# Output products of the first block in pairs, its next operands kept in DRAM unsplit

## The chip, the cores and the metric

The kernel runs on one core of a Trainium2 chip. The metric is the device time of one execution in microseconds (us). Before the change it is 2675.44 us, the median of three runs (2669.7 to 2675.79).

## The reference, cut to what matters

Two blocks follow each other on 512 tokens of 2048 features, all in f32. The first block has two layers; the second has one, with 16 meta tokens ahead of the 512.

```python
for l in range(DEPTH):                       # DEPTH = 2
    h = rmsnorm(x, attn_norm_g[l])
    proj = h @ w_in[l]
    qa, ka, va, ga, cq, ckv, kr, gb = jnp.split(proj, SPLIT_POINTS, axis=-1)
    ya = swa_attention(...) * jax.nn.silu(ga)
    yb = mla_attention(cq, ckv, kr, ...) * jax.nn.silu(gb)
    x = x + jnp.concatenate([ya, yb], axis=-1) @ w_out[l]
return rmsnorm(x, final_norm_g)
...
```

The second block takes that result, normalises it, multiplies by a second input matrix (gates, attention operands, pooling), and ends with a product by a second output matrix.

## The kernel before, in words

**Tiles and products.** Features lie on the 128 partitions, so an activation of 2048 features is 16 operand tiles c of 128x512. A weight tile is 128x1024 in f32: the weights of one output tile t for eight operand tiles (one half u). SP loads it into `wr` (three buffers, or `ws`, two buffers, for weight sums). `load_w_split` (L246) makes two fp32r parts of it: ACT casts it to `wh` (L249), DVE subtracts to get `wl` (`tt`, L129), three buffers each. Every operand is split the same way, and every product is three matmuls: hi by `wh`, lo by `wh`, hi by `wl` (`mm3`, L160). A plain output tile is 2 halves x 8 operands x 3 = 48 matmuls of 512 columns.

**Pairs.** `run_pair` (L346) makes two output tiles at once from seven products of half the columns (8 operands x 3 matmuls each, 168 matmuls of 256 columns), named z, x and y, in place of eight. It needs weight sums, which POOL's accumulating DMAs put into DRAM (`wsd`, `sum_step`, L224, each held back behind a PE instruction), and for each of the eight pairs of operands (n, n+8) an operand set (`t_set`, L327): four half-width operations on DVE and two splits. The sets come from a side task (`t_build`), which reloads the unsplit operands as `tr`. Before the change pairs stand in the second block's input product, except for the first eight gate tiles (`GPLAIN`), and in its output product w_out2 (five pairs).

**The order of the work.** PE runs in the order that the program writes: products, with side tasks (attention heads, norms, operand sets) stepped in between by a clock that counts PE's work. The instructions of the other engines are put in order by a list scheduler, apart from the start, whose order is written by hand. Each engine then works its queue in order. A weight load on SP waits for the split three weight tiles earlier, since that frees its buffer; that split waits for PE to be done with the tile three before it.

**A layer of the first block** (`layer`, L784): the products of w_in in the order cq (three tiles as a group, both halves), ckv, and so on; attention as side tasks; then the product by w_out in 16 output tiles j, the first three as a group. After tile j, DVE adds the old x (`xo`, loaded by SP) to give `xn`, SP stores it, ACT squares it and POOL adds the square up, and the next stage's operand is made at once from `xn`: in layer 0 `hh` (ACT) and `hl` (DVE), in layer 1 `Xh`, `Xl` and an unsplit copy `xr` in DRAM. After the last tile the squares are summed over the partitions by two matmuls (`csum`, from `csh` and `csl`), 33 matmuls into the next stage. In between SP loads `metas` (the meta tokens), whose squares `mq` ACT makes ahead of `csh`.

**The start** is 16 loads of x, a split of each (`hh`, `hl`), a square of each on ACT (`x0q`), which POOL adds up as it comes, and the column sum 111 matmuls into cq, which has 144.

Of the kernel before, what the change touches and what calls it, by code (L numbers as in the profile page):

```python
# [18 lines left out]
P = 128  # L19
# [21 lines left out]
GPLAIN = 8  # L41
# [6 lines left out]
SUMPAIRS = 37  # L48
# [56 lines left out]
def trunk_kernel(ctx, tc, xT, w_in, w_qkv, w_out, w_in2, w_pool, w_aup, w_pup, w_out2, metaT, vec, cst, outT):  # L105
# [283 lines left out]


# [53 lines left out]
    cos_t = slot("cos_t")  # L444
    sin_t = slot("sin_t")
    delta_t = slot("delta_t", F32, 256)
    diag_t = slot("diag_t")
# [3 lines left out]
    def load_consts1():  # L451
        nc.sync.dma_start(cos_t, cst[:, C_COS:C_COS + S])
        nc.sync.dma_start(sin_t, cst[:, C_SIN:C_SIN + S])
        nc.sync.dma_start(delta_t, cst[:, C_DELTA:C_DELTA + 256])
        nc.sync.dma_start(diag_t, cst[:, C_DIAG:C_DIAG + S])

    xrd = tc.dram_tile([P, NC, W], F32, name="xrd")
    xd = [tc.dram_tile([P, NC, S], F32, name=f"xd{i}") for i in range(2)]
# [33 lines left out]
    def swa_pair(i, qps, r, st, nsink, gate, ydst):  # L492
# [10 lines left out]
        for kv in range(2):  # L503
            nc.gpsimd.tensor_scalar(al[:, kv * 256:(kv + 1) * 256], delta_t, -SLOPES[kv * 8 + i], None, op0=ALU.mult)
# [87 lines left out]
    def rope_of(ps, name):  # L592
# [3 lines left out]
        tt(a, ps, cos_t, ALU.mult)  # L596
        for q in range(4):
            src = slice(32 * q, 32 * q + 32)
            d = 32 * (q ^ 1)
            tt(b[d:d + 32], ps[src], sin_t[src], ALU.mult)  # L600
# [50 lines left out]
    def mla_head(h, pr, kr, gate, ydst):  # L651
# [8 lines left out]
        for i in range(NB):  # L660
# [6 lines left out]
            nc.vector.tensor_tensor_reduce(p[:, :n], sc[:, :n], diag_t[:, S - n:], -MLA_SCALE, 1e38, ALU.add, ALU.min,  # L667
# [45 lines left out]
    def plan():  # L713
        for lay in range(DEPTH):
# [17 lines left out]
            for j in range(GRP, NC):  # L732
                for u in range(2):
                    wq.append((w_out[lay, j, u], WCOLS))
        t = 0
        pairs = []
# [47 lines left out]
    def layer(lay, h, rd, x_src, x_dst):  # L784
# [15 lines left out]
        def yget(c):  # L800
            if ys[c] is None:
                need(lambda: y[c] is not None)
                ys[c] = split(y[c], f"y{c}")
                y[c] = None
            return ys[c]
# [46 lines left out]
        res = []  # L852
        for j in range(NC):
            xo = slot("xo")
            nc.sync.dma_start(xo, x_src[:, j, :])
            if j == 0:
                first = run_gemm(2, 8, yget, group=GRP)
            ps = first[j] if j < GRP else run_gemm(2, 8, yget)
            xn = slot("xn")
            tt(xn, ps, xo, ALU.add)  # L860
            nc.sync.dma_start(x_dst[:, j, :], xn)
            sq.add(xn)
            if lay == 0:
                res.append(split_g(xn, vcol(V_ATTN_G + NC * (lay + 1) + j), "h"))
            else:
# [4 lines left out]
                hi = slot("Xh", F32R, W)  # L870
                lo = slot("Xl", F32R, W)
                xr = slot("xr", F32, W)
                nc.scalar.mul(real(xr), halves(xg), g2)
                nc.scalar.mul(halves(xr)[:, :, :M2], halves(metas[:, j * NM:(j + 1) * NM]), g2)
                nc.scalar.dma_start(xrd[:, j, :], xr)
                nc.scalar.mul(real(hi), halves(xg), g2)
                stt(real(lo), halves(xg), g2, real(f32(hi)), ALU.mult, ALU.subtract)
                mt = halves(metas[:, j * NM:(j + 1) * NM])
                nc.scalar.mul(halves(hi)[:, :, :M2], mt, g2)
                stt(halves(lo)[:, :, :M2], mt, g2, halves(f32(hi))[:, :, :M2], ALU.mult, ALU.subtract)  # L880
                res.append((hi, lo))
# [35 lines left out]
    sq0 = SumSq("x0")  # L917
    h = []
    xs = []
    with tc.manual_schedule(engines={mybir.EngineType.Activation, mybir.EngineType.DVE, mybir.EngineType.SP}):  # L920
# [4 lines left out]
        def x_use(c):  # L925
            h.append(split_g(xs[c], vcol(V_ATTN_G + c), "h"))

# [13 lines left out]
        for c in range(1, 4):  # L941
            x_use(c)
            sq0.add(xs[c - 1])
        for c in range(4, 8):
            x_use(c)
            sq0.add(xs[c - 1])
        load_w_split(*raw1)
        for c in range(8, 12):
            x_use(c)
            sq0.add(xs[c - 1])  # L950
        load_w_split(*raw2)
        for c in range(12, NC):
            x_use(c)
            sq0.add(xs[c - 1])
# [534 lines left out]
```

## Time and profile before

| what | value |
|---|---|
| median of three runs | 2675.44 us |
| the profiled execution | 2675.18 us |
| its span | 2673.4 us |
| mean granted clock of PE | 0.992 |
| busy: PE, DVE, ACT, POOL | 98%, 68%, 50%, 19% |
| DMA engines' share, bytes | about 5 tenths, 163 GB/s |
| chain that ended last, by engine | PE 92%, DVE 3%, DMA 2% |

The profiled execution's time is 1.8 us more than its span. Busy shares are means over stages that differ: the products by w_in and w_out run with PE busy all the time, and the idle 2% of PE lies in a few places, at the start, at a layer's end and in the second block. Times inside the profile count from the span's start.

### The profile page before, as it was taken

What the parts mean: (1) busy time and instruction counts of PE and PEld (TensorE: products, weight loads), DVE (VectorE), ACT (ScalarE), POOL (GpSimd) and SP (SyncE); (2) the same over time, 40 slices, a digit from 0 to 9 for tenths busy, and PEclk for the clock granted to TensorE, in tenths of its full rate; (3) what the DMA queues carried; (4) which work ended last, traced back from release to release, by engine and by line L of the source; (5) the groups of instructions that cost most, each with busy time, mean ns of one, the idle gap of its engine ahead of it and who ended that gap; (6) DMA issues with size and microseconds to landing.
All of it is one profiled execution on the core that took longest, in us unless ns stands there. A gap on an engine that the chain in (4) does not pass through costs nothing.

```text
span 2673.4 us, 39297 instructions
## 1 busy us (share of the span) xinstructions
PE 2622.8 (98%) x15169; PEld 2296.0 (86%) x15169; DVE 1804.9 (68%) x2699; ACT 1323.7 (50%) x2192; POOL 513.5 (19%) x501
## 2 busy tenths in 40 slices
PE   7999999999999999999999999999999998999997
PEld 6888888888788888888888999999999986878797
DVE  7767576744467657765466787777777665766786
ACT  5444465532245445555445444335666575733453
POOL 4112123222121212323420122000000031210012
PEclk9999999999999999999999999999999998999998
DMA  5445545577764554458864455545545534466555
GB/s 180 111 145 143 134 119 150 135 218 212 185 160 120 135 138 127 130 146 235 232 187 139 152 178 163 157 159 158 159 154 167 174 115 159 154 215 208 195 175 181
DMA packets 146330, 434.71 MB, mean 163 GB/s; under 512 B 16592, under 2 KB 21072, under 8 KB 146144
## 3 DMA queue, kind: packets, MB, share of 16 engines
q1 hardware_dynamic: 103136, 306.36, 35.6%
q0 software_dynamic: 27312, 97.20, 15.9%
q10 hardware_dynamic: 15696, 28.65, 3.1%
q8 instruction: 119, 1.95, 0.3%
q14 instruction: 67, 0.55, 0.1%
HBM read 382.60 MB, written 127.14 MB: 191 GB/s over the span
## 4 chain that ended last, share of the span: by engine, by line
PE 92%; DVE 3%; DMA 2%; ACT 1%; issue 1%; POOL 1%; ACTq 0%; SPq 0%; DVEq 0%; POOLq 0%
PE mm L160 52%; PE y L160 12%; PE x L160 8%; PE z L160 8%; PE msc L160 1%; PE qn L160 1%; PE sc L160 1%; PE mo L160 1%; PE o L160 1%; PE tp L164 1%; PE kn L160 1%; PE v L160 1%; PE mtp L164 1%; DVE wl L129 1%; PE qr L160 1%
## 5 line engine op out<-in xcount | busy, mean ns | idle before, releaser
L249 ACT CAST wh<-wr 128x1024 fp32r<-128x1024 f32 (+2 forms) x448 | 462.0, 1031 | 683.8 <-PE mm L160 398.8
L129 DVE TENSOR_TENSOR wl<-wr,wh 128x1024 fp32r<-128x1024 f32 (+2 forms) x448 | 568.3, 1272 | 247.5 <-ACT wh L249 234.2
L160 PE MATMUL mm<-hh,wh 128*128 128x512 f32 x1024 | 410.8, 401 | 6.9 <-ACT wh L249 6.6
L160 PE MATMUL mm<-hh,wl 128*128 128x512 f32 x1024 | 405.1, 396 | 4.3 <-DVE wl L129 4.2
L160 PE MATMUL mm<-hl,wh 128*128 128x512 f32 x1024 | 404.9, 395 | 2.7 <-DVE hl L132 2.7
L160 PEld LDWEIGHTS mm<-hh,wl 128*128 128x128 f32 x1024 | 193.4, 189 | 50.5 <-DVE wl L129 5.9
L160 PEld LDWEIGHTS mm<-hh,wh 128*128 128x128 f32 x1024 | 193.8, 189 | 42.8 <-ACT wh L249 6.6
L227 POOL DMA_DIRECT2D wsd<-in_w_in x128 | 88.3, 690 | 732.2 <-PE mm L160 501.3
L160 PEld LDWEIGHTS mm<-hl,wh 128*128 128x128 f32 x1024 | 193.8, 189 | 39.9 <-DVE hl L132 4.6
L249 ACT CAST wh<-ws 128x1024 fp32r<-128x1024 f32 x111 | 116.4, 1048 | 151.9 <-PE y L160 99.8
L160 PE MATMUL y<-t34h,wh 128*128 128x256 f32 (+1 forms) x592 | 167.1, 282 | 0.0
L160 PE MATMUL y<-t34l,wh 128*128 128x256 f32 (+1 forms) x592 | 166.7, 282 | 0.0
L160 PE MATMUL y<-t34h,wl 128*128 128x256 f32 (+1 forms) x592 | 166.6, 281 | 0.0
L129 DVE TENSOR_TENSOR wl<-ws,wh 128x1024 fp32r<-128x1024 f32 x111 | 138.9, 1251 | 21.9 <-ACT wh L249 19.4
L160 PE MATMUL x<-Xl,wh 128*128 128x256 f32 (+1 forms) x512 | 144.6, 282 | 0.0
L160 PE MATMUL x<-Xh,wh 128*128 128x256 f32 (+1 forms) x512 | 144.4, 282 | 0.0
L160 PE MATMUL x<-Xh,wl 128*128 128x256 f32 (+1 forms) x512 | 144.3, 282 | 0.0
L160 PEld LDWEIGHTS y<-t34h,wh 128*128 128x128 f32 x592 | 111.4, 188 | 0.2 <-issue 0.2
L160 PEld LDWEIGHTS y<-t34l,wh 128*128 128x128 f32 x592 | 111.5, 188 | 0.0
L160 PEld LDWEIGHTS y<-t34h,wl 128*128 128x128 f32 x592 | 111.4, 188 | 0.0
L160 PE MATMUL mm<-Xh,wh 128*128 128x512 f32 x256 | 101.9, 398 | 0.0
L160 PE MATMUL mm<-Xh,wl 128*128 128x512 f32 x256 | 100.9, 394 | 0.0
(1023 smaller groups left out, 7057.6 us busy)
## 6 DMA issues: line engine op xcount, KB each, us to landing
wr<-in_w_in SPq DMA_DIRECT2D x256, 512.0 KB, 3.7
wsd<-in_w_in POOLq DMA_DIRECT2D x128, 512.0 KB, 5.3
wr<-in_w_out SPq DMA_DIRECT2D x95, 512.0 KB, 4.6
ws<-wsd SPq DMA_DIRECT2D x37, 512.0 KB, 4.0
wr<-wsd SPq DMA_DIRECT2D x37, 512.0 KB, 3.8
wsd<-in_w_out POOLq DMA_DIRECT2D x20, 512.0 KB, 5.7
xd<-xn SPq DMA_DIRECT2D x32, 256.0 KB, 4.5
sgd<-sga ACTq DMA_DIRECT2D x32, 256.0 KB, 2.2
```

What stands on the lines that cost most here:

```text
L129: nc.vector.tensor_tensor(out, a, b, op)
L160: last_pe[0] = nc.tensor.matmul(out, a, b, start=start, stop=stop, skip_group_check=True).ins
L164: nc.tensor.transpose(out, x, ident)
L227: behind_pe(nc.gpsimd.dma_start(dst, src, **kw))
L249: nc.scalar.copy(hi, raw)
```

## The change

It has five parts. (1) The w_out product of both layers: tiles 0 to 2 as a group, 3 plain, 4 to 13 as five pairs, 14 and 15 plain. Its unsplit operands y are stored to DRAM (`yd`, by POOL) when they are split, and reloaded by `t_build`, now shared by all users, with a shorter yield. (2) The next stage's operands 0 to 13 are stored unsplit (`raw` to `hrd` or `xrd`, by ACT), reloaded by SP as `rr` (eight during tile 14, six during tile 15) and split then. The sum x is written into `xo`. (3) The squares of the input are added on DVE later, the first addition behind a matmul of the cq group; the column sum moves from 111 matmuls into cq to behind all 144. (4) Six plain gate tiles instead of eight. (5) Constants (`cos`, `sin`, `delta`, `diag`) are loaded again at the end of layer 0, which frees their slots before, and `metas` after them.

```diff
-GPLAIN = 8
+GPLAIN = 6
-SUMPAIRS = 37
+SUMPAIRS = 48
...
+    def t_build(ts, get, raw, w):
+        ahead = {}
+        def fetch(n):
+            if n < 8:
+                ahead[n] = []
+                for c in (n, n + 8):
+                    get(c)
+                    ahead[n].append(load(raw[:, c, :], "tr", w))
+        fetch(len(ts))
+        yield 3000
+        while len(ts) < 8:
+            n = len(ts)
+            fetch(n + 1)
+            ts.append(t_set(get(n), get(n + 8), *ahead.pop(n)))
+            yield 6500
...
+        def tile_done(j, xn):
             nc.sync.dma_start(x_dst[:, j, :], xn)
             sq.add(xn)
+            raw = slot("raw", F32, w)
             if lay == 0:
-                res.append(split_g(xn, vcol(V_ATTN_G + NC * (lay + 1) + j), "h"))
+                nc.scalar.mul(raw, xn, vcol(V_ATTN_G + NC + j))
...
+            if lay == 1 or j < NC - 2:
+                nc.scalar.dma_start(rawd[:, j, :], raw)
+            if j >= NC - 2:
+                res[j] = split(raw, "h", w)
+        ts = []
+        start_side(t_build(ts, yget, yd[lay], S))
...
+        for j in range(GRP):
+            xo_load(j)
+        for j, ps in enumerate(run_gemm(2, 8, yget, group=GRP)):
+            plain_out(j, ps)
+        for j in range(GRP, NPLAIN):
+            xo_load(j)
+            plain_out(j, run_gemm(2, 8, yget))
+        need(lambda: len(ts) == 8)
+        for j in range(NPLAIN, NC - 2, 2):
+            xo_load(j)
+            xo_load(j + 1)
+            c = run_pair(ts, 8)
+            t0, t1 = xos.pop(j), xos.pop(j + 1)
+            add_pair(c, t0, t1)
+            tile_done(j, t0)
+            tile_done(j + 1, t1)
...
+        for j in range(NC - 2, NC):
+            xo_load(j)
+            for k in (range(8) if j == NC - 2 else range(8, NC - 2)):
+                res[k] = split(load(rawd[:, k, :], "rr", w), "h", w)
+            plain_out(j, run_gemm(2, 8, yget))
+        if lay == 0:
+            load_consts1()
...
     def scale0():
-        parts = split(sq0.acc, "cs")
-        yield 23000
+        acc = squares[0]
+        for n in range(1, NC):
+            ins = nc.vector.tensor_tensor(acc, acc, squares[n], ALU.add)
+            if n == 1:
+                behind_pe(ins)
+        squares.clear()
+        parts = split(acc, "cs")
+        yield 19000
...
-    start_side(scale0())
+    start_side(scale0(), 12000)
-    start_side(t_build(x2, xrd, W), 6000)
+    start_side(t_build(tset, x2, xrd, W), 6000)
```

The order that results is shown at three places. First, DVE in layer 0's output product where tile 3 ends and the first pair begins (`t12l`, `t34l`: the two splits of an operand set; `xo<-mm,xo`: the addition of tile 3). Before, tile 3's addition stands between weight splits and the next operand's split:

```order
L132 SCALAR_TENSOR_TENSOR hl<-xn,vecs,hh 128x512
L129 TENSOR_TENSOR wl<-wr,wh 128x1024
L129 TENSOR_TENSOR xn<-mm,xo 128x512
L129 TENSOR_TENSOR wl<-wr,wh 128x1024
L132 SCALAR_TENSOR_TENSOR hl<-xn,vecs,hh 128x512
```

Now:

```order
L129 TENSOR_TENSOR xo<-mm,xo 128x512
L129 TENSOR_TENSOR wl<-ws,wh 128x1024
L129 TENSOR_TENSOR ws<-ws,wr 128x1024
L129 TENSOR_TENSOR t_5175<-tr 128x256
L129 TENSOR_TENSOR t_5176<-tr 128x256
L129 TENSOR_TENSOR t_5175<-tr,t_5175 128x256
L129 TENSOR_TENSOR t_5176<-tr,t_5175 128x256
L129 TENSOR_TENSOR t12l<-t_5175,t12h 128x512
L129 TENSOR_TENSOR t34l<-t_5176,t34h 128x512
L129 TENSOR_TENSOR t_5189<-tr 128x256
```

The sets 6 and 7, the last two that the first z product uses, come behind the addition of tile 3, a weight split and a weight sum.

Second, SP's queue where layer 0 ends. Before:

```order
L194 DMA wr<-in_w_in 128x1024 x2
L861 DMA xd_94<-xn 128x512
L855 DMA xo<-in_xT 128x512
L194 DMA wr<-in_w_in 128x1024 x2
L861 DMA xd_94<-xn 128x512
L970 DMA metas<-in_metaT 128x256
```

Now, from the load of the sixth weight tile of the next layer on:

```order
L194 DMA wr<-in_w_in 128x1024
L392 DMA rr<-hrd 128x512
L392 DMA xo<-in_xT 128x512
L392 DMA rr<-hrd 128x512
L194 DMA wr<-in_w_in 128x1024
L899 DMA xd_93<-xo 128x512
L392 DMA rr<-hrd 128x512 x5
L486 DMA cos<-in_cst 128x512
L486 DMA sin<-in_cst 128x512
L486 DMA delta<-in_cst 128x256
L486 DMA diag<-in_cst 128x512
L1045 DMA metas<-in_metaT 128x256
```

The first row's load waits for the split of the third weight tile of that layer, the second `wr` for that of the fourth. Reload 7, the x of tile 15 and reload 8 stand between them; the store of tile 15, five reloads, four constants and the metas stand behind both.

Third, DVE at the same place. Before, the last split of the layer's operands is followed by the squares of the metas and the column sum's split:

```order
L129 TENSOR_TENSOR xn<-mm,xo 128x512
L129 TENSOR_TENSOR wl<-wr,wh 128x1024
L132 SCALAR_TENSOR_TENSOR hl<-xn,vecs,hh 128x512
L974 TENSOR_REDUCE metasq<-mq 128x16
L129 TENSOR_TENSOR csl<-xq,csh 128x512
```

Now (the first `wl` is that of the fourth weight tile of layer 1):

```order
L129 TENSOR_TENSOR hl<-rr,hh 128x512 x3
L129 TENSOR_TENSOR wl<-wr,wh 128x1024
L129 TENSOR_TENSOR hl<-raw,hh 128x512
L129 TENSOR_TENSOR xo<-mm,xo 128x512
L129 TENSOR_TENSOR hl<-rr,hh 128x512 x6
L129 TENSOR_TENSOR hl<-raw,hh 128x512
L1049 TENSOR_REDUCE metasq<-mq 128x16
L129 TENSOR_TENSOR csl<-xq,csh 128x512
```

The addition of tile 15 moved behind a weight split that waits for PE's first weight tile of layer 1, and the column sum's split behind six reloaded operands and that addition.

## Rows read from the trace of the kernel before

**Rows 1.** The page: the span, and section 1, busy time of each engine.

```profile
span 2673.4 us, 39297 instructions
PE 2622.8 (98%) x15169; PEld 2296.0 (86%) x15169; DVE 1804.9 (68%) x2699; ACT 1323.7 (50%) x2192; POOL 513.5 (19%) x501
```

**Rows 2.** Windows: us, PE, PEld, DVE, ACT, POOL busy (instructions), PEclk, DMA share, GB/s.

```profile
600.00:700.00 100.00, 100.00 (x431) 80.72 (x430) 43.51 (x36) 29.31 (x36) 25.34 (x23) 1.00 0.77 212
2540.00:2640.00 100.00, 100.00 (x852) 100.00 (x851) 78.95 (x96) 51.36 (x62) 17.14 (x14) 1.00 0.56 179
```

**Rows 3.** Timeline of the start: us, length, engine, line, instruction, idle time before it.

```profile
8.92 26.73 POOL L422 TENSOR_TENSOR x0q<-x0q 128x512 f32<-128x512 f32 x15 [6.51 <-ACT x0q L136]
6.47 0.72 ACT L463 ACTIVATE hh<-xs,vecs 128x512 fp32r<-128x512 f32 x1
7.61 0.71 ACT L463 ACTIVATE hh<-xs,vecs 128x512 fp32r<-128x512 f32 x1
28.96 0.80 PE L160 MATMUL mm<-hh,wl 128*128 128x512 f32 x1 [3.20 <-DVE wl L129]
45.87 0.39 PE L160 MATMUL csum<-csh,ones_r 128*128 128x512 f32 x1
54.12 0.69 DVE L129 TENSOR_TENSOR cq<-mm,r 128x512 f32<-128x512 f32 x1 [1.07 <-PE mm L160]
59.41 0.69 DVE L129 TENSOR_TENSOR csl<-cqnsq,csh 128x512 fp32r<-128x512 f32 x1 [3.22 <-ACT csh L151]
61.55 0.39 PE L160 MATMUL csum<-csh,ones_r 128*128 128x512 f32 x1
```

**Rows 4.** Groups of instructions on DVE and ACT: total, mean ns, idle before; 540:690, 2400:2480.

```profile
L129 DVE TENSOR_TENSOR wl<-wr,wh 128x1024 fp32r<-128x1024 f32 x27 | 33.1, 1224 | 34.3 <-ACT wh L249 34.2
L249 ACT CAST wh<-wr 128x1024 fp32r<-128x1024 f32 x27 | 28.4, 1051 | 105.6 <-PE mm L160 59.3 <-issue 46.3
L129 DVE TENSOR_TENSOR t<-tr 128x256 f32<-128x256 f32 x4 | 1.7, 420 | 1.4 <-DMA tr<-mgd 1.4
```

**Rows 5.** Timeline and window at the head of the last product (w_out2).

```profile
2480.05 1.23 DVE L129 TENSOR_TENSOR wl<-wr,wh 128x1024 fp32r<-128x1024 f32 x1 [2.24 <-ACT wh L249]
2481.19 0.68 DVE L129 TENSOR_TENSOR t12l<-t,t12h 128x512 fp32r<-128x512 f32 x1
2482.39 0.68 DVE L129 TENSOR_TENSOR ym<-mm,sgl 128x512 f32<-128x512 f32 x1
2483.22 0.77 PE L160 MATMUL mm<-mg0h,wh 128*128 128x512 f32 x1 [4.11 <-DVE ym L129]
2482.00:2490.00 8.00, 6.78 (x18) 5.39 (x19) 5.26 (x9) 1.24 (x2) 0.00 (x0) 0.57 0.95 314
```

**Rows 6.** Timeline of SP's queue, DVE, ACT and PE where layer 0 ends.

```profile
696.35 0.69 DVE L129 TENSOR_TENSOR xn<-mm,xo 128x512 f32<-128x512 f32 x1 [3.54 <-PE mm L160]
697.07 0.33 SPq L861 DMA_DIRECT2D xd<-xn  x1
697.45 0.42 SPq L970 DMA_DIRECT2D metas<-in_metaT  x1
703.80 0.42 ACT L136 ACTIVATE mq<-metas 128x256 f32<-128x256 f32 x1 [5.48 <-DMA metas<-in_metaT]
704.78 0.50 PE L160 MATMUL csum<-csh,ones_r 128*128 128x512 f32 x1 [0.89 <-ACT csh L151]
```

**Rows 7.** DMA issues, whole run: operation, count, KB each, median us to landing.

```profile
wr<-in_w_in SPq DMA_DIRECT2D x256, 512.0 KB, 3.7
sgd<-sga ACTq DMA_DIRECT2D x32, 256.0 KB, 2.2
xo<-xd SPq DMA_DIRECT2D x16, 256.0 KB, 6.3
tr<-xrd SPq DMA_DIRECT2D x16, 264.0 KB, 4.1
```

**Rows 8.** Window where layer 1 ends; columns as in the windows above.

```profile
1340.00:1400.00 60.00, 60.00 (x261) 48.58 (x261) 37.24 (x54) 29.73 (x51) 15.56 (x9) 1.00 0.58 173
```

More of the change, by code (lines that the diff above doesn't have):

```diff
@@ L388, in pair_out, with load, add_pair @@
         return t0, t1
+    def load(src, name, n=S, queue=nc.sync):
+        t = slot(name, F32, n)
+        queue.dma_start(t, src)
+        return t
+    def t_build(ts, get, raw, w):
[13 more added lines that the diff above has]
+            yield 6500
+    def add_pair(c, t0, t1):
+        lo, hi = slice(0, HN), slice(HN, S)
+        tt(t0[:, lo], c[0], t0[:, lo], ALU.add)
+        for t, k, op in ((t0[:, hi], 1, ALU.add), (t1[:, lo], 2, ALU.subtract), (t1[:, hi], 3, ALU.subtract)):
+            tt(t, c[k][0], t, ALU.add)
+            if op == ALU.add:
+                tt(t, c[k][1], t, ALU.add)
+            else:
+                tt(t, t, c[k][1], ALU.subtract)
     def rsqrt_m(out, m, n):
@@ L713, in plan @@
     def plan():
+        pairs = []
         for lay in range(DEPTH):
@@ L731, in plan @@
             grouped(w_out[lay], 0, GRP)
-            for j in range(GRP, NC):
+            w = w_out[lay]
+            for j in range(GRP, NPLAIN):
                 for u in range(2):
-                    wq.append((w_out[lay, j, u], WCOLS))
+                    wq.append((w[j, u], WCOLS))
+            for j in range(NPLAIN, NC - 2, 2):
+                blocks = (w[j, 0], w[j, 1], w[j + 1, 0], w[j + 1, 1])
+                wq.extend(pair_steps(len(pairs), *blocks, WCOLS))
+                pairs.append(blocks)
+            for j in range(NC - 2, NC):
+                for u in range(2):
+                    wq.append((w[j, u], WCOLS))
         t = 0
-        pairs = []
         for kind, i in SEQ2:
@@ L851, in layer @@
             sq2 = SumSq("xg")
[L852 to L860, printed above, removed]
+        res = [None] * NC
+        rawd, w = (hrd, S) if lay == 0 else (xrd, W)
+        def tile_done(j, xn):
             nc.sync.dma_start(x_dst[:, j, :], xn)
             sq.add(xn)
+            raw = slot("raw", F32, w)
             if lay == 0:
-                res.append(split_g(xn, vcol(V_ATTN_G + NC * (lay + 1) + j), "h"))
+                nc.scalar.mul(raw, xn, vcol(V_ATTN_G + NC + j))
             else:
@@ L914, in layer @@
         return res, rn
-    sq0 = SumSq("x0")
+    squares = []
     h = []
@@ L953, in trunk_kernel @@
             x_use(c)
-            sq0.add(xs[c - 1])
-        sq0.add(xs[NC - 1])
     xs = None
@@ L1177, in trunk_kernel @@
     mg = {}
-    def load(src, name, n=S, queue=nc.sync):
-        t = slot(name, F32, n)
-        queue.dma_start(t, src)
-        return t
-    def t_build(get, raw, w):
-        ahead = {}
-        def fetch(n):
-            if n < 8:
-                ahead[n] = [load(raw[:, c, :], "tr", w) for c in (n, n + 8)]
-        fetch(len(tset))
-        yield 3000
-        while len(tset) < 8:
-            n = len(tset)
-            fetch(n + 1)
-            tset.append(t_set(get(n), get(n + 8), *ahead.pop(n)))
-            yield 8000
     def u_order(t):
```

66 lines of the change are left out of this document (30 added, 36 removed).

## The prediction

> **What bounds the kernel now.** I read the busy times first [rows 1]: TensorE (PE) has work in 2622.8 of 2673.4 us, so time can leave only with matmuls, and any new wait of PE is paid in full. The profiled execution took 2675.18 us, within 0.3 us of the median of the three runs, so I sum against 2675.2. A difference under 0.3% (8 us) I call no change. Next come the cadences [rows 2]: in the output product of layer 0 PE issues 431 matmuls of 512 columns in 100 us, 0.232 us each; in the pairs of the last product 852 of 256 columns, 0.1174 us each. In both stretches PE is busy throughout at clock 1.00, while DVE has 43.5 and 79 of 100 us: a pair hides its DVE work. The third view is the places where PE stands today [rows 3, 5, 6]: each is a product whose operand is late, and these price the new ones.
>
> **Pairs.** Two plain tiles are 2 x 48 matmuls, 96 x 0.232 = 22.27 us; a pair is 168 x 0.1174 = 19.72. That saves 2.55, ten times in two layers: 25.5 us. Gate tiles 6 and 7 become an eleventh pair: 2.6. Together **-28.1**. The weight sums for it are POOL's DMAs, which PE does not wait for today either; PE is fully busy with DMA at 0.77 [rows 2], so I cost them at nothing; without that cover they show as later landings, which the upper bound takes.
>
> **The start.** Today POOL's 15 additions run from 8.92 to 35.65, and within them PE waits up to 3.20 us for a weight split [rows 3]. Without them DVE keeps up with ACT, which gives an operand every 1.14 us (6.47 to 7.61). By that pace the first weight tile is used up and the second split by 16.9, and the other 120 matmuls of the group take 27.8 us: the end at 44.7, against 54.1 (the last cq scaling waits for PE until 54.12). That is 9.4 us earlier. The 15 additions on DVE (0.69 each) fit under PE. But the column sum of x0 now comes behind all 144 matmuls, at 44.7. Today it runs at 45.87 and the split for the second column sum ends at 60.10, 14.2 us on, of which DVE gave 1.07 to waiting for PE. With 13.1 us the same chain ends at 57.8; PE has 33 matmuls (7.7 us) to fill and stands 5.4. The second sum then runs at 57.8 instead of 61.55: **-3.7**. Bounds: -9.4 if the chain is hidden, 0 if ACT's pace does not carry DVE.
>
> **The first group and the first pair of each layer's output product.** In the group, DVE builds three operand sets (4 x 0.42 + 2 x 0.68 = 3.0 us each, [rows 4, 5]) and a weight split ahead of the split of operand 12. Their work is spread over the group's first half, 72 matmuls or 16.7 us, in which DVE also has the splits of operands 8 to 15 and of three weight tiles; no row shows that, and I take 2 us of wait per layer, half of the 4.11 that [rows 5] show for such a queue, **+4** (0 to 8). The first pair wants set k 0.35 us x k after the end of tile 3 (three matmuls a set). In DVE's order the addition of tile 3, a weight split (1.22) and a weight sum stand before sets 6 and 7, and SP issues the two reloads of set 7 behind the store of that tile: 0.7 + 1.2 + 1.2 (the sum, taken as long as a split of the same shape) + 3.0 + 2.3 = 8.4 us after tile 3, needed at 2.5. So PE waits 5.9 per layer, **+12** (8 to 14). The row that shows this happening today is the head of w_out2 [rows 5]: a weight split and two set splits stand before an operand, and PE stands 4.11 us.
>
> **The end of layer 0.** T is the end of tile 15. SP works its queue in order: today it issues the store of the last tile at 697.07, 0.7 us after the addition that it waits for, and the metas right behind it at 697.45 [rows 6]. Each weight load waits for the split three tiles earlier, and that for PE. The reloads are put between these loads. Reload 7 stands behind a load that waits for the end of tile 15: split 1.2, issue 0.4 each, issued at T+2.0; I take 4.1 us to landing, the row of the nearest load, an unsplit operand read back by SP [rows 7]; cast and split end at T+7.4. Its place in the first w_in tile is T+4.9, and PE stands 2.4. That tile ends at T+8.0. Only then comes a weight split (1.2) that SP waits for, and behind it on DVE the split of tile 14 and the addition of tile 15, at T+10.6; the store, reloads 9 to 13, four constants and the metas are issued after it, the metas when reload 10 has landed (eight transfers are outstanding at most): T+16.3. Today the metas take 6.35 us from issue to use [rows 6]; ACT squares them ahead of the cast for the column sum, so the cast and split end at T+23.7. PE reaches that sum 33 matmuls into the layer, here at T+10.1, and stands 13.3. Today the same wait is 1.1 (0.89 on the cast, the rest on the split). **+14.6**.
>
> **The end of layer 1.** Today it costs nothing: 60 of 60 us are busy [rows 8]. The order is worse here: even tile 15's own x stands behind a weight load that waits for the end of the first gate tile's first half, T+8.0. Issued at T+9.6, landed 6.3 later [rows 7], added at T+16.6; reloads 9 to 13 follow the store, the first is split at T+22.6, and the second half of the tile wants it at T+8.7. The column sum comes three operands into that half and needs tile 15's squares through ACT and POOL, T+27.8, against T+7.7 undisturbed. **+20**.
>
> On the price of a landing, a page has another view. The Trainium skill, "DMA: Bandwidth & Descriptors", section on the anatomy of one DMA, gives a fixed cost near 2.0 us plus the bytes over 436 GB/s, for transfers that POOL issues; for 256 KB that is an estimate of 2.6 us, and by it the two layer ends would cost 8.5 and 13.3 and the sum would be 2694. The trace does not agree for this kernel: such loads of SP land in 4.1 to 6.3.
>
> **The clock.** After the wait of 4.11 us the granted clock is at the lower level (1.2 GHz): 0.57 in the mean of 2482 to 2490, 18 matmuls in 6.78 us where 0.232 each would be 4.2 [rows 5]. So a wait of that size costs 2.6 more. I count five: start, two first pairs, two layer ends: **+13** (0 to 21).
>
> **Constants, yields, squares.** The reloaded constants are in the end of layer 0. The shorter yields of the operand sets in the later stages change nothing there if the sets are ready as today; a late set 7 of the gate pairs would cost at most what a first pair costs, 5.9.
>
> **Sum.** -28.1 - 3.7 + 4 + 12 + 14.6 + 20 + 13 = +31.8: **2707 us**. With the fastest landing of a 256 KB transfer in the rows, 2.2 us [rows 7], the layer ends cost 7.3 and 11.8, the first pairs 8, four clock falls 10.4, the groups nothing, the start gains 9.4: 2675.2 + 0.0, no change. With 6.3 us they cost 21 and 26, the pairs 14, the groups 8, eight clock falls 21, the start nothing: +62, 2737.
>
> **The rivals.** *The reloads come in time*, faster. Its condition: the reloads and the metas are in SBUF before PE asks, although SP's queue is in order; it decides at a landing that leaves reload 7 before T+3.6 and the metas before T+8. Then the layer ends cost nothing, and -28.1 - 3.7 + 4 + 12 + 3 x 2.6 = -8.0: 2667. If the sets of the first pair are on time as well, 2643. For it: PE never stands at the end of layer 1 today, and a new load waits for no arithmetic in itself. Against it: metas, alone behind one store, already cost PE 1.1 us [rows 6]. *Quick landings*, no change: all transfers near 2.2 us, 2675, as worked out; the store of SBUF tiles by ACT shows that figure, the loads do not. *The DMA engines saturate*, slower than forecast: pair stages add the stores and reloads of y and of the next operands to a share of 0.77; landings of 6.3 everywhere, 2737.
>
> **Chances and range.** My forecast (slower, layer ends binding) has 0.50 and the saturated case 0.10. No change has 0.15: quick landings, or half the waits. The reloads in time have 0.25: both in-order queues speak against them, but my walk through the queues has many steps. The forecast's own range is 2690 to 2725. To leave out no more than 2 in 10, the range goes down to 2660 and up to 2732.
>
> **What would show it.** Right: PE idle over 10 us within 30 us of each layer's last w_out tile, ended by the cast for csum or by a split of a reloaded operand, with SP's reloads issued after that tile; 5 to 7 us of idle in the first z product of each layer; 852 matmuls per 100 us in the pairs; the first cq group done near 45. Wrong: PE busy across both layer ends, or pairs slower than 0.1174 a matmul, or the first cq group still ending near 54.

## The result, and the profile after

The changed kernel takes 2761.51 us (median of four runs, 2755.95 to 2764.74) against 2673.78 beside it: 1.0327 of the time before, interval 1.0314 to 1.034. That is slower, as forecast, but 54 us above the forecast of 2707 and outside its range. The four runs lie 9 us apart, and the profiled execution is the longest of them, 2764.74 us; its span is 2762.8. First the page: span, busy times, granted clock in 40 slices.

```profile
span 2762.8 us, 41611 instructions
PE 2631.1 (95%) x15961; PEld 2335.1 (85%) x15961; DVE 1925.3 (70%) x2923; ACT 1389.0 (50%) x2279; POOL 535.4 (19%) x564
PEclk9999999999899999999988999999999998999998
```

Against [rows 1], PE is idle for 131.7 us instead of 50.6. It is also busy for 8.3 us more, although eleven pairs took 11 x 2.55 = 28 us of matmuls out. So PE is busy some 36 us longer than these matmuls took before. The mean granted clock is 0.972; before it was 0.992. The waits of PE say for what it stood (waited for, us in total, times, longest):

```profile
PE mm L160 <- ACT hh L151: 23.3, 6, 10.6
PE csum L160 <- ACT csh L151: 21.6, 3, 13.0
PE z L160 <- ACT t12h L151: 17.8, 4, 7.1
...
PE z L160 <- DVE wl L129: 6.2, 2, 4.6
PE mm L160 <- ACT y12h L151: 5.4, 2, 2.9
```

The operands of the next stage, the column sum, the operand sets of the first pair, a weight split within the pairs, an operand in the group: each a place that the prediction named, except the weight splits in the pairs. Windows of layer 0's pairs and of both layer ends (columns as in [rows 2]):

```profile
600.00:640.00 40.00, 38.47 (x325) 38.26 (x325) 28.16 (x34) 19.19 (x24) 11.84 (x15) 1.00 1.03 340
640.00:680.00 40.00, 35.35 (x276) 35.14 (x276) 26.51 (x30) 17.41 (x23) 12.49 (x13) 0.91 0.97 294
720.00:760.00 40.00, 24.48 (x82) 18.09 (x83) 15.52 (x21) 14.22 (x22) 3.87 (x4) 0.73 0.50 155
1440.00:1480.00 40.00, 22.56 (x66) 15.23 (x65) 19.10 (x30) 16.82 (x32) 6.88 (x6) 0.64 0.44 135
```

In the pairs the DMA engines' share has risen from 0.77 [rows 2] to 0.97 and 1.03, so there is no room left, and PE loses time in a stage that was fully covered. At the layer ends (window 720 to 760 and 1440 to 1480) PE works 24.5 and 22.6 of 40 us, at a clock of 0.73 and 0.64. The DMA view of 600 to 690 shows who fills the engines (GB/s in 40 slices; queue: packets, MB, share of 16 engines; issues: count, KB, median us to landing):

```profile
GB/s 335 323 389 413 422 289 280 269 282 257 394 276 314 419 421 400 295 357 155 157 265 394 320 261 265 266 267 395 335 162 290 336 288 375 368 368 202 295 277 371
...
q0 software_dynamic: 2985, 10.85, 48.2%
q1 hardware_dynamic: 5336, 15.18, 45.5%
...
wsd<-in_w_in POOLq DMA_DIRECT2D x22, 512.0 KB, 8.4
wr<-in_w_out SPq DMA_DIRECT2D x13, 512.0 KB, 8.3
xd<-xo SPq DMA_DIRECT2D x9, 256.0 KB, 8.6
xo<-in_xT SPq DMA_DIRECT2D x9, 256.0 KB, 12.8
```

The same view of the kernel before, 600 to 680:

```profile
q0 software_dynamic: 1590, 5.75, 35.3%
...
wr<-in_w_out SPq DMA_DIRECT2D x12, 512.0 KB, 5.1
wsd<-in_w_in POOLq DMA_DIRECT2D x11, 512.0 KB, 5.0
```

q0 is POOL's queue, which carries the weight sums (`wsd`). They are stepped once per weight tile, in three of four. A plain weight tile lasts 24 x 0.232 = 5.57 us of PE, a pair's 19.72 / 7 = 2.8: in pairs, sums and weights are both asked for twice as fast. A pair also takes seven weight tiles where two plain tiles take four, so each output product now issues 35 sums instead of 24 and 20. In the two views 22 sums instead of 11 fall into about the same time; a sum lands after 8.4 us instead of 5.0, a weight load after 8.3 instead of 5.1.

The time between marks in PE's timeline (first y0 matmul of a layer's output product, last matmul of tiles 3 and 14; tile 13's end taken as 11.13 us, one plain tile, ahead of tile 14's; the last row ends at PE's last column sum) gives a ledger, in us. The five last columns are experiments told below.

| stage | before | after | no sums in w_out | no pairs | six plain first | mended | mended, sums back |
|---|---|---|---|---|---|---|---|
| start and w_in, layer 0 | 515.5 | 511.5 | 511.8 | 511.4 | 512.1 | 511.6 | 512.1 |
| group and tile 3, layer 0 | 46.4 | 54.9 | 51.9 | 46.2 | 55.7 | 48.3 | 48.3 |
| tiles 4 to 13, layer 0 | 111.7 | 121.9 | 108.9 | 110.8 | 105.8 | 101.4 | 106.2 |
| tile 14 to end of w_in, layer 1 | 519.4 | 544.8 | 538.7 | 541.6 | 544.0 | 521.5 | 534.7 |
| group and tile 3, layer 1 | 46.3 | 50.7 | 49.4 | 46.3 | 50.8 | 49.9 | 48.3 |
| tiles 4 to 13, layer 1 | 111.2 | 123.4 | 114.7 | 111.0 | 108.9 | 103.6 | 109.8 |
| tile 14, layer 1, to the end | 1308.6 | 1340.3 | 1354.7 | 1335.7 | 1335.6 | 1322.9 | 1333.8 |

**The first pair**, in three engines' timelines of layer 0 (SP, DVE, PE):

```profile
568.36 0.91 SPq L392 DMA_DIRECT2D tr<-yd  x2
...
567.23 0.68 DVE L129 TENSOR_TENSOR xo<-mm,xo 128x512 f32<-128x512 f32 x1
567.83 1.22 DVE L129 TENSOR_TENSOR wl<-ws,wh 128x1024 fp32r<-128x1024 f32 x1
569.08 2.17 DVE L129 TENSOR_TENSOR ws<-ws,wr 128x1024 f32<-128x1024 f32 x1
...
577.53 0.43 DVE L129 TENSOR_TENSOR t<-tr 128x256 f32<-128x256 f32 x1 [3.30 <-DMA tr<-yd]
...
572.96 0.58 PE L160 MATMUL z<-t12h,wh 128*128 128x256 f32 x1 [4.07 <-ACT t12h L151]
579.63 0.58 PE L160 MATMUL z<-t12h,wh 128*128 128x256 f32 x1 [5.15 <-ACT t12h L151]
```

Sets 6 and 7 stand behind tile 3's addition, a weight split and a weight sum, as forecast; the sum takes 2.17 us, not 1.2, and the reloads of set 7 land 9 us after their issue (568.36 to about 577.4), not 4.1. PE stands 9.2 us in place of 5.9, and its clock falls: 0.83 in the mean of 560 to 600.

**The end of layer 0**, SP's queue, then ACT's, then PE (tile 15 ends at 711.7):

```profile
729.15 0.33 SPq L194 DMA_DIRECT2D wr<-in_w_in  x1
730.36 0.32 SPq L899 DMA_DIRECT2D xd<-xo  x1
730.77 2.59 SPq L392 DMA_DIRECT2D rr<-hrd  x5
...
736.38 0.33 SPq L1045 DMA_DIRECT2D metas<-in_metaT  x1
...
735.68 3.30 ACT L151 CAST hh<-rr 128x512 fp32r<-128x512 f32 x5 [6.78 <-DMA rr<-hrd]
738.89 0.62 ACT L136 ACTIVATE xq<-xo 128x512 f32<-128x512 f32 x1
...
741.41 0.60 ACT L151 CAST csh<-xq 128x512 fp32r<-128x512 f32 x1
742.06 0.80 PE L160 MATMUL csum<-csh,ones_r 128*128 128x512 f32 x1 [12.97 <-ACT csh L151]
```

The forecast chain is there row by row: SP held by a weight load until 729.15, behind it the store of tile 15, five reloads and the metas. It ended at T+30.4 instead of T+23.7. The square of tile 15 (`xq`), which the column sum needs, stands on ACT behind the casts of five reloaded operands.

PE's timeline at the start, then at the end of layer 1:

```profile
44.19 0.39 PE L160 MATMUL csum<-csh,ones_r 128*128 128x512 f32 x1
55.66 0.79 PE L160 MATMUL csum<-csh,ones_r 128*128 128x512 f32 x1 [3.22 <-ACT csh L151]
...
1438.71 0.79 PE L160 MATMUL mm<-hh,wh 128*128 128x512 f32 x1 [6.06 <-ACT hh L151]
1455.15 0.79 PE L160 MATMUL mm<-hh,wh 128*128 128x512 f32 x1 [10.56 <-ACT hh L151]
1467.31 0.80 PE L160 MATMUL csum<-csh,ones_r 128*128 128x512 f32 x1 [5.41 <-ACT csh L151]
```

The start went as forecast: both column sums earlier than in [rows 3], the output product of layer 0 4.0 us earlier. Layer 1's end, which cost nothing before [rows 8], has three waits.

### The profile page after: what moved, and what is told of

The parts are those of the page before. It is cut to its first block, busy times and chain, and to the rows that moved or that the text cites. A ratio compares the mean times of both kernels' runs of the same rounds, so it can differ in the third digit from the quotient of the medians.

```text
span 2762.8 us, 41611 instructions
## 1 busy us (share of the span) xinstructions
PE 2631.1 (95%) x15961; PEld 2335.1 (85%) x15961; DVE 1925.3 (70%) x2923; ACT 1389.0 (50%) x2279; POOL 535.4 (19%) x564
## 4 chain that ended last, share of the span: by engine, by line
PE 45%; DMA 3%; DVE 3%; ACT 1%; issue 1%; POOL 0%; SPq 0%; ACTq 0%; DVEq 0%; POOLq 0%
PE mm L160 13%; PE y L160 13%; PE x L160 9%; PE z L160 8%; DMA xd<-xo 1%; DMA rr<-xrd 1%; DVE wl L129 1%; PE zB L160 1%; DVE out L1414 0%; PE so L160 0%; PE pw L160 0%; PE zA L160 0%; ACT wh L249 0%; DMA xo<-xd 0%; DMA vr<-vd 0%
## 5 line engine op out<-in xcount | busy, mean ns | idle before, releaser
L160 PE MATMUL mm<-hh,wh 128*128 128x512 f32 x1248 | 504.2, 404 | 30.2 <-ACT hh L151 23.3
L160 PE MATMUL mm<-hl,wh 128*128 128x512 f32 x1248 | 497.3, 398 | 1.4 <-DVE hl L129 0.9
L160 PE MATMUL mm<-hh,wl 128*128 128x512 f32 x1248 | 496.1, 397 | 0.6 <-DVE wl L129 0.5
L160 PE MATMUL y<-t34h,wh 128*128 128x256 f32 (+1 forms) x768 | 217.7, 283 | 2.8 <-DVE ab L129 2.7
L160 PE MATMUL y<-t34l,wh 128*128 128x256 f32 (+1 forms) x768 | 217.1, 283 | 0.0
L160 PE MATMUL x<-hh,wh 128*128 128x256 f32 (+1 forms) x528 | 148.9, 282 | 0.0
L160 PE MATMUL x<-hl,wh 128*128 128x256 f32 (+1 forms) x528 | 148.7, 282 | 0.0
L160 PE MATMUL x<-hh,wl 128*128 128x256 f32 (+1 forms) x528 | 148.6, 281 | 0.0
L129 DVE TENSOR_TENSOR ws<-ws,wr 128x1024 f32<-128x1024 f32 x96 | 136.2, 1419 | 3.2 <-DMA wr<-in_w_out 0.2
L160 PE MATMUL z<-t12h,wh 128*128 128x256 f32 (+1 forms) x384 | 109.7, 286 | 17.8 <-ACT t12h L151 17.8
```

Of the source, the lines that this page charges most:

```text
L129: nc.vector.tensor_tensor(out, a, b, op)
L160: last_pe[0] = nc.tensor.matmul(out, a, b, start=start, stop=stop, skip_group_check=True).ins
```

## The experiments

Each kernel differs from the changed one by the edit shown, except the start alone and the six gates alone, which are the kernel before with one part of the change; their diffs are against the kernel before. Where no interval is given there is one run, and one trace gives a stage to no better than some 5 us (shown below); the kernel before, run beside them, took 2672.05 to 2677.35.

**No weight sums in the output products** (held from the first w_out tile of a layer to its tile 15).

```diff
-            if last_pe[1] > 12 and last_pe[1] % 4 and presum:
+            if last_pe[1] > 12 and last_pe[1] % 4 and presum and not hold[0]:
...
+        hold[0] = True
...
+        hold[0] = False
```

> Edit: the changed kernel, but POOL issues no weight sums while the w_out product of a layer runs (they wait until it is over). DMA theory (the sums come once per weight tile, so twice as fast in pairs; the DMA engines at 0.99 make every landing late): the DMA share inside the pairs falls from 0.99 to 0.6 or 0.7, PE's waits inside the pairs (13.6 us) go to under 2, the wait in the first z product and at the layer ends shrinks towards the forecast sizes, and the time falls from 2761 to about 2715 (2700 to 2730). Queue theory (only the order of the in-order queues counts, the load of the DMA engines does not): first z and layer ends stay within 10% of 17.8 and 42 us, and the time stays above 2740.

Measured: 2747.37 us. By the column sum of layer 1 it is 35 us ahead of the changed kernel (1432.2 against 1467.3): tiles 4 to 13 take 13.0 and 8.7 us less. But the program's rest takes 18 us more. Windows of layer 0's pairs and of the second block:

```profile
600.00:640.00 40.00, 40.00 (x341) 40.00 (x340) 31.21 (x37) 20.82 (x28) 6.35 (x4) 1.00 0.65 213
...
1700.00:1800.00 100.00, 94.91 (x773) 94.30 (x772) 67.81 (x80) 36.64 (x43) 22.75 (x36) 0.97 0.98 302
```

With a share of 0.65, PE runs 341 matmuls in 40 us of pairs, the forecast cadence of 852 in 100; with 1.03 and 0.97 it was 325 and 276. But 88 sums are now issued behind layer 1's output product, where the changed kernel has 18 and the kernel before none. They lie in pairs of the second block, whose share rises to 0.98 and where PE loses 5 of 100 us. So the pairs are slower by the sums, and holding these back moves their cost on: the pairs behave as the DMA theory said, and the time misses its 2700 to 2730.

**Reloads issued by POOL**, with the sums and without.

```diff
-                res[k] = split(load(rawd[:, k, :], "rr", w), "h", w)
+                res[k] = split(load(rawd[:, k, :], "rr", w, nc.gpsimd), "h", w)
```

> Edit: the changed kernel, but the 14 reloads of the next stage's operands are issued by POOL instead of SP. Queue theory: reloads no longer stand behind SP's weight loads (though on POOL they stand behind paced weight sums), SP reaches the metas sooner; PE's waits for hh at the layer ends (23 us) fall below 12, time 2735 to 2750. DMA theory: the waits for hh stay near 23, time 2755 to 2765.

> Edit: both edits together (no weight sums during w_out, reloads issued by POOL). DMA theory: hardly better than the kernel without the sums alone (within 6 us). Queue theory: at least 15 us better than without the sums alone, since then nothing stands ahead of the reloads. If each has its part, about 2700 (2690 to 2715), and what is left at the layer ends is the column sum's wait for the metas, which still stand behind tile 15's store.

Measured: 2744.86 and 2745.82. The first of these times lies where the queue theory put it, but the waits for reloaded operands, which that theory had under 12 us, are 17.7 against 23.3. The layer ends (tile 15 to the column sum) take 28.8 and 34.9 us in the first, 29.6 and 30.2 in the second, against 31.5 and 38.9; 9.6 and 8.1 before. The wait for the column sum is still 13.8 and 13.6 us. Taking the reloads out of SP's queue is not enough. The Trainium skill, "DMA: Bandwidth & Descriptors", section "Issuing engines are not separate DMA queues", says that transfers of SP, ACT and POOL end on the same 16 engines and that another issuer saves only the time to issue. The two ends agree as far as they go: in the first run they are 2.7 and 4.0 us shorter, out of 22 and 31. But one in-order queue was exchanged for another, since in POOL's the reloads stand behind sums that wait for PE (4.31 us at 700.84).

Tiles 4 to 13 of layer 0 took 116.2 us in the first run and 116.4 in the one with x and metas ahead (below), against 121.9. No edit reaches that stage in either; the order on every engine is the same there, and only the wait of 4.65 us (PE, 660.37) is missing. So 5.5 of the 13.0 us that the run without sums gained there may be the scatter of single executions, and the sums' price in these pairs lies between 7.5 and 13.

**The reload without pairs.** All 16 tiles plain, operands 0 to 13 still through DRAM; y is not stored.

```diff
-            for j in range(GRP, NPLAIN):
+            for j in range(GRP, NC):
...
-            c = run_pair(ts, 8)
...
+            for d in range(2):
+                xo_load(j + d)
+                plain_out(j + d, run_gemm(2, 8, yget))
```

> Edit: the changed kernel with all tiles of w_out plain (no operand sets, no stores of y), so the next stage's operands are still stored, reloaded and split late: part 2 alone, with the start and the six gate tiles of the change. DMA share in w_out then as before the change (about 0.8). Queue theory: the layer ends cost nearly what they cost in the changed kernel (35 to 42 us of idle), time 2700 to 2715. DMA theory: they cost about half (20 us), time 2685 to 2697.

Measured: 2719.72. Output products as before (46.2 and 110.8), layer ends 30.1 and 34.5 us: 20.5 and 26.4 more than before, with no pair anywhere near. Two of PE's waits:

```profile
720.03 0.79 PE L160 MATMUL csum<-csh,ones_r 128*128 128x512 f32 x1 [12.23 <-ACT csh L151]
1410.84 0.79 PE L160 MATMUL mm<-hh,wh 128*128 128x512 f32 x1 [8.59 <-ACT hh L151]
```

So part 2 of the change costs its 47 us by its order, as the queue theory had it, and more than the 2700 to 2715 that it named; the pairs add 6 to that.

**x of the last tiles, constants and metas ahead of the reloads**; then the same without sums in w_out (one behind each weight tile in w_in instead, every second one in the second block) and with the reloads on POOL.

```diff
         for j in range(NC - 2, NC):
             xo_load(j)
+        if lay == 0:
+            load_consts1()
+            load_metas()
+        for j in range(NC - 2, NC):
...
-        if lay == 0:
-            load_consts1()
```

> Edit: the changed kernel, but x of tiles 14 and 15, the four constants and the metas are loaded (and the metas squared) ahead of the 14 reloads, so the addition of tile 15 no longer stands behind the next layer's weight splits. Chain theory (the layer ends are set by the chain x of tile 15, its addition, its store, then five reloads, constants and metas, each a round trip): the wait of the column sum in layer 0 falls from 13.0 to under 5 us, the wait of 10.6 us for a reloaded operand in layer 1 to under 5; from tile 15's end to the column sum layer 0 takes 20 instead of 31.5, layer 1 24 instead of 38.9; time 2735 (2728 to 2745). Landing theory (the reloads land late under the load of the DMA engines, whatever is ahead of them): both ends within 4 us of the changed kernel's, time 2754 or more.

> Edit: the one before, with the reloads issued by POOL, no weight sums in w_out, and the sums spread otherwise: one per weight tile while w_in runs, one per second weight tile in the second block (so that they don't pile up there). Both theories together: layer ends near 15 us each, 4 to 13 as pairs 105 to 112 us (98.6 without any wait), no weight split waited for in the second block; time 2690 (2675 to 2705). If the sums only move their cost, the rest of the program is again 15 us or more longer than in the kernel before.

Measured: 2755.54 and 2731.45. In the first, the column sum of layer 0 still waits 12.25 us. ACT's queue there:

```profile
735.00 3.25 ACT L151 CAST hh<-rr 128x512 fp32r<-128x512 f32 x5 [7.00 <-DMA rr<-hrd]
738.16 0.62 ACT L136 ACTIVATE xq<-xo 128x512 f32<-128x512 f32 x1
...
740.23 0.62 ACT L151 CAST csh<-xq 128x512 fp32r<-128x512 f32 x1 [0.18 <-POOL xq L457]
```

The metas are no longer in the way, and nothing is gained (ends of 35.4 and 34.3 us against 31.5 and 38.9): the five casts that wait for the last reloads hold tile 15's square, whatever lies behind it. The prediction's own wording, that the metas' landing sets the column sum, falls here. Both mends with the sums away bring the ends to 18.2 and 25.1 us; then 8.0 us of wait for the column sum and 9.4 for a reloaded operand are left. The time misses its 2675 to 2705: 62 sums are left for the second block, and the rest of the program takes 19 us more than before, the case that the expectation named for sums that only move their cost.

**The start alone** (part 3 on the kernel before) and **the six gate tiles alone** (part 4; the last two lines of the cut, beside one more pair of sums), eleven runs each.

```diff
-        parts = split(sq0.acc, "cs")
-        yield 23000
+        acc = squares[0]
+        for n in range(1, NC):
+            ins = nc.vector.tensor_tensor(acc, acc, squares[n], ALU.add)
...
-GPLAIN = 8
+GPLAIN = 6
```

> Edit: the kernel before the change with the new start alone (squares of x added on DVE later, column sum behind all 144 matmuls). Forecast by the steps of the prediction: 3.7 us less, of which a clock fall may give back 2.6: ratio 0.9990 (0.9975 to 1.000). In the changed kernel's trace the first matmul of layer 0's w_out came 4.0 us earlier than before. Rival: it is lost later, ratio 1.000.

> Edit: the kernel before the change with six plain gate tiles (gates 6 and 7 as a pair, one more pair of weight sums) alone. Forecast: 2.6 us less, ratio 0.9990. Rival: the operand sets of that pair are not ready, PE waits for the last of them, and it gains nothing or costs up to 6 us (ratio 1.000 to 1.002): the side task still yields 8000 per set here, where the change made it 6500.

Measured: 2671.36 us, ratio 0.999 (0.9981 to 0.9999), and 2674.62, ratio 1.0003 (0.9994 to 1.0011). The start gives 2 to 3 us (0.3 to 5.1 by the interval). The eleventh pair gives at most 1.6 of its 2.6: from layer 1's column sum on PE is idle 3.5 us longer, 1.5 of it a wait for the pair's last operand set (1444.05), as the rival had it. In the changed kernel, whose side task yields less per set, that wait is absent.

**Six plain tiles ahead of the pairs** (four pairs per layer).

```diff
-            for j in range(NPLAIN, NC - 2, 2):
+            for j in range(6, NC - 2, 2):
```

> The changed kernel with six plain tiles ahead of the pairs instead of four, so four pairs per layer instead of five; all else as changed. Theory: the first pair's z product waits because its last operand sets stand behind tile 3's addition and a weight split in DVE's order, whatever the DMA load. Two more plain tiles (22 us) let the sets finish: the waits in the first z (9.2 and 8.6 us) go, tiles 4 to 13 take about 110 and 113 us instead of 121.9 and 123.4, of which one pair less costs 2.6, and the program ends near 2740. Rival: the sets are late because the DMA engines are full; then the waits come back in later pairs and tiles 4 to 13 stay at 118 or more, the end near 2755.

Measured: 2729.35, better than forecast. Giving up one pair per layer makes the program 32 us faster. Windows of layer 0:

```profile
600.00:640.00 40.00, 37.70 (x306) 37.50 (x305) 28.60 (x33) 18.57 (x24) 12.11 (x13) 0.96 0.97 306
640.00:680.00 40.00, 40.00 (x314) 38.78 (x313) 26.18 (x33) 19.09 (x24) 13.31 (x14) 1.00 1.03 332
```

The share is as full as in the changed kernel, and PE loses 2.3 us in the pairs instead of 15.4. Tiles 4 to 13 take 105.8 and 108.9 us, 5 to 8 more than two plain tiles and four pairs at their cadences. So the full engines take little from a pair whose sets are ready; they hurt more by making late reloads later.

**The sums spread**: one behind each weight tile in w_in, none in layer 0's output product, one of three in layer 1's, three of four after that.

```diff
-            if last_pe[1] > 12 and last_pe[1] % 4 and presum:
+            if last_pe[1] > 12 and pace[0](last_pe[1]) and presum:
```

> The changed kernel with the weight sums spread: one behind each weight tile in the products by w_in instead of three of four, none in layer 0's output product, one of three in layer 1's, then three of four as changed. Nothing moves into the second block. Theory (the sums in the pairs fill the DMA engines, and a plain product by w_in has room): layer 0's tiles 4 to 13 take about 109 us as without sums, layer 1's about 118, the two w_in stages stay at 511 and 490, the rest at 1279, and the program ends near 2735. Rival (the sums cost what they cost, wherever they are put): the w_in stages grow by what the pairs gain, or the second block does as it did when the sums were merely held back (+18), and the end stays near 2750.

Measured: 2745.01, 10 above the forecast. Tiles 4 to 13 took 108.6 and 115.3 us and the w_in stages 511.6 and 489.8, as the theory has it: plain products do have room. But the rest took 1287.1 instead of 1279, with one wait of 5.28 us for a weight split (1619). 38 sums were still left for the second block, against 18 in the changed kernel.

**All mended, and the column sum later.** On top of six plain tiles, spread sums, x and metas ahead, reloads by POOL and a later start of the operand sets:

```diff
             parts = split(sq.acc, "cs")
-            yield 6000
+            yield 16000
...
-            ps = run_gemm(2, 8, x2)
+            if i == 0:
+                gps = run_gemm(2, 8, x2, group=GRP)
+            ps = gps[i] if i < GRP else run_gemm(2, 8, x2)
```

Then the same with all 14 reloads in tile 14, and, on the first of the two, `yield 22000`; last, that one with the sums back at three of four throughout.

> All mended at once: four pairs after six plain tiles, sums spread (none in the pairs of layer 0, one of three in layer 1), reloads issued by POOL, x and metas ahead; and new: the column sum of the next stage some 88 matmuls into it instead of 33, and the second block's first three gate tiles as a group, so that operands 8 to 15 are wanted 72 matmuls into the stage instead of 24. Theory: what is left of the layer ends (18.2 and 25.1 us in the run with x and metas ahead and reloads on POOL, 9.6 and 8.1 before) is the order: the column sum and the upper operands are asked for before a landing, a cast and a split can be done. Then both ends show under 3 us of idle, and the program ends between 2655 and 2670, below the kernel before. Rival: the transfers themselves are too slow beside the weights; then the wait comes back at operand 8 of the group, 72 matmuls on, and the end stays above 2690.

> As the run before, but all 14 reloads issued during tile 14 instead of eight there and six during tile 15, so that none stands behind tile 14's square in POOL's queue. If the late six still set the layer ends there, this takes 3 to 8 us off each; if the ends are already free of waits, the two runs are equal within 0.3%.

> The run with the late sums of squares, and the column sum of the next stage later still, behind about all 144 matmuls of its first group (88 there). Theory: what is left at the layer ends there (waits of 4.35 and 7.75 us for the cast of the column sum, and the slow clock behind each) is the order of the sums again: tile 15's addition and its squares come only after the last reloaded operands on DVE and ACT, 26 to 30 us behind the layer's last matmul, and PE asks at 20. Asked for at 33, both waits go, and the program is 10 to 16 us faster than the 2682.2 of that run: 2666 to 2672, 0.996 to 0.999 of the kernel before. Rival: the cq scalings and the first gates then wait for the norm that comes later, and PE stands as long one tile further on: within 4 us of 2682.

> The run beside it, with the weight sums put back where the change has them: three of four weight tiles throughout, in the pairs too. It prices the full DMA engines by themselves, with the operand sets in time and the layer ends mended. If the full engines alone slow the pairs, tiles 4 to 13 take 106 and 109 us (as with six plain tiles first) against 101.4 and 103.6, and the layer ends, whose reloads then share the engines with the sums, wait again: 10 to 25 us more. If the sums only hurt by making late sets later, the two runs differ by less than 6 us.

Measured: 2682.19; 2686.79; 2677.63, ratio 1.0018 (1.0009 to 1.0027) over eleven runs; 2711.7. The first misses its forecast of 2670 at most: waits of 4.35 and 7.75 us for the column sum are left. Reloads in one lot, expected to take 3 to 8 us off each end, make that no better (5.47 and 11.85). Asked for later again, the sum of layer 0 is not waited for at all and that of layer 1 for 3.06 us; so the order was the cause there. But of the 10 to 16 us expected only 4.6 came, and that against a single run: small waits for reloaded operands (0.4 to 1.5 us) stand in their place. What the sums cost follows from the last two. Windows of the mended kernel, and then with the sums back:

```profile
560.00:640.00 80.00, 80.00 (x587) 75.83 (x586) 62.34 (x76) 39.46 (x51) 11.57 (x7) 1.00 0.59 198
680.00:720.00 40.00, 37.66 (x159) 29.13 (x158) 25.77 (x32) 18.92 (x28) 6.18 (x8) 1.00 0.42 145
```

```profile
560.00:640.00 80.00, 78.24 (x555) 73.77 (x554) 58.27 (x71) 37.58 (x49) 22.67 (x24) 0.98 0.97 297
680.00:720.00 40.00, 31.72 (x121) 23.63 (x119) 16.18 (x21) 13.98 (x21) 11.52 (x17) 0.87 0.83 276
```

34 us in all: 4.8 and 6.2 in the pairs, 13 and 11 behind them. In the pairs that is the price of the full engines. Behind them it is not theirs alone, for POOL's queue has the reloads behind the sums. The first eight reloads of layer 0 in the mended kernel, then one of them with the sums back:

```profile
665.18 4.26 POOL L393 DMA_DIRECT2D rr<-hrd  x8
```

```profile
683.94 0.89 POOL L228 DMA_DIRECT2D wsd<-in_w_in  x1 [3.55 <-PE mm L160]
684.50 0.91 POOL L393 DMA_DIRECT2D rr<-hrd  x1
```

With the sums back the eighth goes out at about 692 instead of 669. How much of the 24 us is the engines and how much this order was not tried; in the changed kernel, where SP issues the reloads, taking the sums away shortened the ends by 3.5 and 3.4 us. No version with pairs in the first block went below the kernel before; the start alone is the only one that did.

## Why the prediction was right and wrong

**Right:** the direction and the places. The start came as forecast (-3.7, measured -4.0), by luck in part: the second column sum ran at 55.66, 2.1 us earlier than forecast, and the measured gain has a clock fall in it that was forecast apart. The first pair waits for the operands that were named, behind the rows of DVE and SP that were named. At the layer ends the queues' order costs 20.5 and 26.4 us by itself; 14.6 and 20 plus two clock falls were forecast. How the landing enters the bounds of the ends (7.3 and 11.8, 21 and 26) the prediction does not show; 6.3 us in place of 4.1 in the steps that it does show gives about 19 and 22.

**The step that failed** is the one on the weight sums: "PE is fully busy with DMA at 0.77, so I cost them at nothing". They are stepped by weight tiles, not by time, and a pair uses weight tiles twice as fast. The share went to 1.0 and landings from 5 to 8.4 us and more. The sign that the prediction gave for being wrong came: 325 pair matmuls in 40 us are 0.123 us each, not 0.1174. Without sums in the output products the program is 35 us ahead at layer 1's column sum, 30 if the 5.5 us of scatter are left out. That is over half of the 54 us missed. It overlaps with the late sets: where these are in time, the sums cost the pairs 4.8 and 6.2 us instead of 13.0 (or 7.5) and 8.7, and with the sums in place two more plain tiles ahead of the pairs took 32 us off the program. The rival of the saturated engines, at a chance of 0.10, named the full engines but not the sums: it laid them to the stores and reloads of y and of the next operands, and with all of these, but without the sums, the share in the pairs is 0.65. Its time of 2737 was short too, since it took 6.3 us for the slow landing.

**The sum, term by term.** Tiles 4 to 13: -25.5 for ten pairs, 12 for the first ones and 5.2 for their clock were forecast, -8.3 in all; measured +10.2 and +12.2. In layer 0 the 23 us above 111.7 - 12.75 are 9.2 in the first z product, 6.2 of other waits and some 7.6 of slow matmuls. Layer ends: 34.6 and 5.2 forecast, 21.9 and 30.8 measured. The groups: 4 forecast, with the wait of 4.11 in [rows 5] as its measure; measured 8.5 and 4.4. Six gates: -2.6 forecast; alone at most 1.6, and in the changed kernel no gain can be seen (1279.2 us from layer 1's column sum on, 1278.2 before, 1279.9 with the start alone, which does not touch that stage).

**The clock** was put at five falls of 2.6 us, +13. The price of one fall was right, the count was not. Each layer has seven new waits of 2 us or more, in the group, the first z, the later pairs and two or three at the end. Between 530 and 1480 us the granted clock stands at 0.50, the lower level (1.2 GHz), in eleven stretches, where it stood at 1.00 throughout before. PE is at work in them for 57.4 us, half of which, 28.7, is the price: 2.6 each. What the other 7 of the 36 us of busy time are was not traced. In the mended kernel PE is busy for 2610.1 us; the nine pairs take 23 us out, which would leave 2599.8. Of the 10 us between, the stretches at the lower level account for 5.

**A part of the mechanism was named wrongly:** the metas. They came late, as forecast, but loading them early changed nothing; tile 15's square, behind the casts of reloaded operands on ACT, was due at the same time: in the changed kernel POOL adds it up until 740.9, and ACT waits 0.31 us for the metas until 741.1. What stays open is the 14 us that the mended kernel still loses from tile 14 of layer 1 on: PE is idle for 10 us more there than before (31.4 against 21.2), in small waits for several things, and which of the parts brings each was not tried.

## What to carry to other kernels

Work that is stepped by loop iterations speeds up with the loop: before shortening a stage, ask what else is issued per step of it, and take the DMA share times the new pace. An operand that is parked in DRAM comes back through in-order queues, so count not its landing but what every queue has in front of its load, its cast and its split, and place the first use behind that. Where a stage must first be prepared, one more step of the slow form in front of it can be worth more than the fast form: a pair given up per layer gained 32 us.

## What the runs showed of the hardware

The engines' share reached 1.0 at 294 to 340 GB/s in windows of 40 us. The Trainium skill, "DMA: Bandwidth & Descriptors", section "Where 436 GB/s comes from", puts the ceiling of the ports at 435 GB/s and names about 358 as HBM's share for one core. Single slices of 2.25 us here reached 422 GB/s, so the lower figure is no ceiling for this kernel, while its full windows stay below both. The bytes are not all alike: from 600 to 690 POOL's queue took 48.2% of the engines' time for 10.85 MB and SP's 45.5% for 15.18 MB, which over 90 us is 4.0 against 2.7 us of all engines per MB.

Twenty-eight us of matmuls were taken out of PE and its busy time grew by 8. In the first block of the changed kernel the granted clock fell to the lower level eleven times, each time at a wait of PE, and a fall cost 2.6 us in the mean. Short waits were followed by it too: in the mended kernel PE waited 0.40 and 1.14 us for `y11` (until 1205.93), and from 1207 to 1210 the granted clock was 0.50.
